# Forty matmuls that nobody reads, at four places of a one-core decoder layer

## The chip, the cores and the metric

The kernel runs on one core of a Trainium2 chip. The metric is the device time of one execution in microseconds (us). The kernel before was timed three times; the median is 1254.13 us (1252.01 to 1255.34). One further execution was profiled, and it is the one whose rows are quoted.

## The reference

One decoder layer on 1024 tokens of width 1024, all in float32. A mixer and a gated MLP follow each other, each between two RMS norms:

```python
h = _rms_norm(x, norm_pre_mix)
mix, v_first = _hybrid_mixer(h, ...)          # RWKV-7 heads beside a causal 31-tap convolution
x = x + _rms_norm(mix, norm_post_mix)
h = _rms_norm(x, norm_pre_ffn)
f = _conv_ffn(h, ...)                         # (gelu(conv3(h @ up)) * conv3(h @ up')) @ down
x = x + _rms_norm(f, norm_post_ffn)
...
# inside the mixer
p = h @ w_in                                  # 1024 -> 1024 (GLU) + 3 * 512 + small ones
y = _wkv7(r, decay, k, v, -kk, kk * a)        # a recurrence over the tokens, 8 heads of 64
c = silu(layer_norm(causal_dwconv(glu(u))))   # 512 channels, 31 taps
mix = concatenate([rwkv_out, c]) @ w_out      # 1024 -> 1024
```

## The kernel before, in words

The tokens are worked in two halves of 512, and the recurrence in four quarters of 256 (each four chunks of 64). Every matrix product with a weight is done as three matmuls on rounded parts: a weight tile is loaded by a DMA from SyncE's queue (line 184), ScalarE rounds it into `wh`, GpSimd subtracts to get `wl` (line 167), and TensorE accumulates `wh*hi`, `wh*lo` and `wl*hi` (lines 330 to 352). All matmuls go through one helper, so they carry line 140; transposes by TensorE carry line 155.

The program is written as streams with priorities (line 60): `rwkv` (1000) comes first, then `top` (the norm behind the first mixer half), `norm`, `conv` and last `proj` (the large products). A planner simulates all engines over time and lays out the order of every engine: at each moment an engine gets the ready instruction with the best priority. So `proj` matmuls fill the time that the recurrence leaves on TensorE. On the chip each engine then runs its list strictly in order, apart from weight loads. A matmul's accumulator is a PSUM bank taken by `bank(tag)`: there are two with the tag `pb`, two `pe`, one `pc`, and three fixed ones (`xs[0]`, `xs[1]`, `Y`). A bank is given out in rotation, and the next user waits until its last reader is done.

Four places matter here.

- **The second half's first transposes.** `channels` (line 273) takes four rows of 128 normalised tokens and turns them so that channels lie on partitions. For the second half it fills one bank per 128 channels: eight banks in turn, with tags pe, pb, pb, pe, pb, pb, pe, pb, four transposes of 128 columns each (line 287). ScalarE scales each bank into `hi` (line 292), VectorE makes `lo` (line 294), and that read frees the bank. After the eight banks stand the second half's first projections (`project(1, hs, "k0 k1 w r0 r1")`, line 1382). The first half runs the same helper with banks of two rows each.
- **The two output projections.** `w_out` (line 778) rounds the mixer's result into pairs (line 791), then makes four column blocks `ch` of 256. Each block uses two banks for 512 tokens and 96 matmuls of 256 columns. Block 0 uses `pb` banks, block 1 the banks `xs`. `evac` multiplies each bank into a tile (line 797), squares it for the norm's sum (ScalarE, line 803) and stores the tile to DRAM as `mixd` (line 805).
- **Behind the first output projection.** `w_out(0, ...)` is called at line 1394. The following `norm_ffn` (line 1400, stream `top`) loads `mixd` back in pieces into tiles `pt` (line 885), adds the residual (line 886), squares (line 887), and does its transposes as products with diagonal matrices `kk` in `pb` banks. At the same time the recurrence of the fourth quarter runs (`prepare(3)`). Its `bonus` (line 585) holds products with the constant block matrix in plain float32.
- **Ahead of the second output projection.** Nine products of the MLP's first matrix for the first half (`ffn_pair`, line 1410) fill TensorE up to `w_out(1, ...)` at line 1413. Their banks are read by `taps` (lines 910 to 919).

`self.lw` (line 249) is a constant of 96 partitions, written once near the start (ScalarE line 253, GpSimd line 255) and only read afterwards.

Of the kernel before, what the change touches and what calls it, by code (L numbers as in the profile page):

```python
# [22 lines left out]
P = 128  # L23
# [3 lines left out]
HALF = 512  # L27
# [73 lines left out]
class Trunk:  # L101
# [37 lines left out]
    def mm(self, out, lhsT, rhs, start=True, stop=True, skip=False):  # L139
        return self.nc.tensor.matmul(out, lhsT, rhs, start=start, stop=stop, skip_group_check=skip)  # L140

    def after(self, i, first):

        self.tc.add_manual_dep(
            i.ins, first.ins.name,
            mybir.DependencyInfo(mybir.DependencyClass.NoSync, mybir.DependencyReason.DATA),
            reason="the bank's first matmul clears it")
# [122 lines left out]
        self.ccarry = cp.tile([P, 4, 32], F32, name="ccarry")[:, :, :CONV_W - 1]  # L270


    def channels(self, rows, gname, hs, toks, tags=("pn",), diags=None):


        nc = self.nc
        n = len(rows) * P
        per = 512 // n
        for b, k0 in enumerate(range(0, KT, per)):
            ps = self.bank(tags[b % len(tags)])  # L280
            for i in range(per):
                k = k0 + i
                for t, row in enumerate(rows):
                    o = (k % 4) * P
                    out, src = ps[:, i * n + t * P:i * n + (t + 1) * P], row[k // 4][:, o:o + P]
                    if diags is None:
                        self.transpose(out, src)
                    else:
                        self.mm(out, src, diags[t])
            parts = [(self.par(gname, k0 + i), ps[:, i * n:(i + 1) * n], *hs[k0 + i]) for i in range(per)]  # L290
            for g, pv, hi, lo in parts:
                self.mark_hi = nc.scalar.activation(hi[:, toks], pv, AF.Copy, scale=g)
            for g, pv, hi, lo in parts:
                self.mark_lo = nc.vector.scalar_tensor_tensor(lo[:, toks], pv, g, hi[:, toks].bitcast(F32), ALU.mult, ALU.subtract)
# [483 lines left out]
    def w_out(self, h, mixr, co, behind=None):  # L778
        nc = self.nc
        if h == 0:  # L780
            acts = self.pairs("m")
        else:
            acts = []
            for _ in range(2):
                two = [self.tl("l8", [P, 4, HALF], F32R) for _ in range(2)]
                acts += [tuple(b[:, k] for b in two) for k in range(4)]
        with ExitStack() as gate:
            if behind is not None:
                gate.enter_context(self.tc.issue_after(behind.ins))
            for k in range(KT):  # L790
                self.split(*acts[k], mixr[:, k] if k < 4 else co[k - 4])

        def evac(ch, pss, post):
            for b, ps in enumerate(pss):
                o = self.tl("t2", [P, 512])
                with self.tc.high_priority():
                    nc.vector.tensor_tensor(  # L797
                        o.rearrange("p (t c) -> p t c", t=2), ps.rearrange("p (t c) -> p t c", t=2),
                        post.unsqueeze(1).broadcast_to([P, 2, 256]), ALU.mult)
                    for t in range(2):  # L800
                        tt = 4 * h + 2 * b + t
                        c = slice(t * 256, (t + 1) * 256)
                        nc.scalar.activation(ps[:, c], ps[:, c], AF.Square, accum_out=self.ssq[:, tt, ch:ch + 1])
                r = h * HALF + b * 256
                nc.sync.dma_start(
                    self.mixd[r:r + 256, ch * 256:(ch + 1) * 256].rearrange("(t p) c -> p t c", t=2),
                    o.rearrange("p (t c) -> p t c", t=2))

        for ch in range(4):
            post = self.tl("po", [P, 256])  # L810
            nc.sync.dma_start(post, self.a["post_mix"][:, ch * 256:(ch + 1) * 256].broadcast_to([P, 256]))
            pss = self.xs if ch == 1 else [self.bank("pe" if h and ch == 2 else "pb") for _ in range(2)]
            for k2 in range(KT // 2):
                wh, wl = self.weight(self.a["w_out"][ch, k2], [P, 2, 256], (self.mix, "ca", "ck") if h else None)
                if ch == 1 and k2 == 0:
                    mark = self.load
                for t in range(4):
                    for kk in range(2):
                        k = 2 * k2 + kk
                        hi, lo = acts[k]  # L820
                        s = slice(t * P, (t + 1) * P)
                        out = pss[t // 2][:, (t % 2) * 256:(t % 2 + 1) * 256]
                        start = k == 0 and t % 2 == 0
                        i = self.mm(out, hi[:, s], wh[:, kk], start=start, stop=False, skip=True)
                        if start:
                            first = i
                        elif k == 0 and kk == 0:
                            self.after(i, first)
                        self.mm(out, hi[:, s], wl[:, kk], start=False, stop=False, skip=True)
                        self.mm(out, lo[:, s], wh[:, kk], start=False, stop=k == KT - 1, skip=True)  # L830
            evac(ch, pss, post)
        return mark
# [26 lines left out]
    def norm_ffn(self, h, row, piece, hs, ahead=2, tags=("pn",), dg=None, pool=None):  # L859
# [38 lines left out]
        if ahead == 4:  # L898
            channels(0)
            yield  # L900
        channels(1)

    def taps(self, h, i, br, ps, acc):
# [219 lines left out]
    def ffn_down(self, acts):  # L1123
# [18 lines left out]
        def product(banks, src, wt, start, after, then=lambda j: None, held=(), soon=True):  # L1142
            ops, n = [], HT - len(held)
            for j in range(HT):
                with first():
                    hi, lo = self.pair("a", self.h1p)
                    self.split(hi, lo, src(j))
                    then(j)
                wh, wl = self.weight(wt(j), [P, 512], held=self.h1p if j % 2 else None) if j < n else held[j - n]
                op = (hi, wh), (hi, wl), (lo, wh)  # L1150
                if j >= n:
                    ops.append(op)
                else:
                    for t in range(4):
                        mms(banks[t], t, op, start and j == 0, j == HT - 1)

            ins = []
            for t in range(4):
                for i, op in enumerate(ops):
                    ins += mms(banks[t], t, op, False, i == len(held) - 1)  # L1160
                with first() if soon else ExitStack():
                    after(t)
            self.chain(ins)
# [101 lines left out]
    def mixer(self, sts):  # L1265
# [39 lines left out]
        def prepare(q):  # L1305

            c = lambda i: chunk(q - 1, i) if q else None
            f = lambda i: step(self.finish, q - 1, i, mixes[(q - 1) // 2]) if q else None

            c(0)  # L1310
            if q == 2:
                c(1)
                f(0)
            step(self.scores, q, 0)
            step(self.scores, q, 1)
            if q == 2:
                c(2)
                c(3)
                f(1)
                c = f = lambda i: None  # L1320
            c(1)
            step(self.keys, q)
            step(self.inverses, q)
            if q != 2:
                step(self.bonus, q)
            c(2)
            if q % 2:
                weave(self.merge(W[q]))
            c(3)
            f(0)  # L1330
            f(1)
            if q in (0, 2):
                weave(self.merge(W[q]), quarter(q + 1))
# [11 lines left out]

        def channels(rows, hs):
            with self.stream("norm"):
                self.channels(rows, "pre_mix", hs, slice(0, HALF), ("pe", "pb", "pb"))

        cut = lambda t: (t[:, :512], t[:, 512:])  # L1350
        with self.stream("norm"):
            two = [self.tl("l8", [P, 2, D]) for _ in range(2)]
            rows = [cut(two[t // 2][:, t % 2]) for t in range(4)]
            with self.stream("first"):
                self.load_rows(0, rows)
            hs = self.pairs("h")
# [7 lines left out]
        with self.stream("norm"):  # L1364
            two = self.tl("mixr", [P, 2, D])
            rows = [cut(two[:, t]) for t in range(2)]
# [10 lines left out]
        project(0, hs, "u2 u3")  # L1377
        hs = self.pairs("h")
        channels(rows, hs)
        mixes[0] = self.tl("mixr", [P, 4, HALF])  # L1380
        prepare(1)
# [10 lines left out]
        conv(1, 1, sts[0]["normed"])  # L1392
        with self.stream("proj"):
            self.w_out(0, mixes[0], [sts[0]["co", i] for i in range(4)])
        mixes[1] = self.tl("mixr", [P, 4, HALF])
        prepare(3)
        with self.stream("top"):
# [90 lines left out]
```

## Time and profile before

| | |
|---|---|
| timed executions | 1252.01, 1255.34, 1254.13 us; median 1254.13 us |
| the profiled execution | 1257.58 us, of which the span from first to last instruction is 1255.8 us |
| mean granted TensorE clock | 0.985 of full speed |
| TensorE matmul busy | 1210.4 us (96%), 8424 matmuls |
| VectorE, ScalarE, GpSimd busy | 899.8, 729.1, 507.1 us |

How to read the rows further below. Times are microseconds from the start of the span. A row of the timeline gives start, duration, engine (PE is TensorE, DVE VectorE, ACT ScalarE, POOL GpSimd, SPq the queue of SyncE), line, operation, output<-inputs by the program's names with buffer numbers left out, shape, and the number of instructions merged into the row. In brackets stands the idle time before it and who ended it. A row of the windows gives for a stretch of time its length, then for PE, PE's weight loads, DVE, ACT and POOL the busy time with the count of instructions, then the granted TensorE clock (1.00 is full), the share of the DMA engines, and GB/s. PE durations overlap, since matmuls are pipelined; what one matmul costs is the distance from start to start.

### The profile page before, as it was taken

Reading aid. Unit: us, or ns where it says so; the run is one execution under the profiler, and the core shown is the slowest. Engines: PE = TensorE matmul, PEld = TensorE weight load, DVE = VectorE, ACT = ScalarE, POOL = GpSimd, SP = SyncE. Lnnn points to the kernel's source line nnn. Section 1 sums busy time; section 2 is a strip of 40 time slices with the busy share of each in tenths; the row PEclk is TensorE's granted clock in tenths of the full one; section 3 lists DMA queues with packets and bytes.
Section 4 is the critical chain, followed back from the end, with each engine's and each line's share of the span. In section 5 each row is a group of like instructions: output and inputs, shape, how many; then the busy total and the mean of one; then the engine's idle time right before and its main releaser. Section 6 shows DMA issues by size and latency. Waiting matters only on the chain.

```text
span 1255.8 us, 22979 instructions
## 1 busy us (share of the span) xinstructions
PE 1210.4 (96%) x8424; PEld 988.9 (79%) x8424; DVE 899.8 (72%) x1558; ACT 729.1 (58%) x1515; POOL 507.1 (40%) x447
## 2 busy tenths in 40 slices
PE   5999999999999998999999999999999999999997
PEld 4767777787778876778889888888888888888885
DVE  5285998898669989998640555666656679479667
ACT  7563564565955676466762576876555566554451
POOL 4343330001103331344563399998888850000002
PEclk9999998999999989999999999999999999999999
DMA  7644442333343353222364798894322335336413
GB/s 243 177 131 137 129 135 64 97 128 119 114 128 91 97 178 110 75 80 85 104 186 118 271 323 293 298 315 153 82 74 81 101 134 166 95 117 219 134 52 134
DMA packets 102912, 180.97 MB, mean 144 GB/s; under 512 B 14896, under 2 KB 21424, under 8 KB 102800
## 3 DMA queue, kind: packets, MB, share of 16 engines
q1 hardware_dynamic: 102800, 179.51, 45.6%
q8 instruction: 66, 1.08, 0.4%
q14 instruction: 46, 0.38, 0.1%
HBM read 138.44 MB, written 41.03 MB: 143 GB/s over the span
## 4 chain that ended last, share of the span: by engine, by line
PE 62%; DVE 6%; ACT 2%; issue 1%; DMA 1%; POOL 1%; POOLq 0%; DVEq 0%; ACTq 0%
PE pb L140 27%; PE xs L140 16%; PE pe L140 14%; PE Y L140 2%; PE pc L140 2%; DVE pc L431 2%; DMA pt<-mixd 1%; PE pc L155 1%; PE pe L155 0%; DVE x L1120 0%; DVE m L167 0%; DVE sub L606 0%; DVE nrow L1136 0%; DVE dw L608 0%; DVE t L797 0%
## 5 line engine op out<-in xcount | busy, mean ns | idle before, releaser
L167 POOL TENSOR_TENSOR wl<-wr,wh 128x512 fp32r<-128x512 f32 (+1 forms) x175 | 230.0, 1316 | 219.4 <-ACT wh L167 191.3
L140 PE MATMUL pb<-h,wh 128*128 128x512 f32 (+3 forms) x720 | 230.1, 399 | 2.5 <-ACT wh L167 1.0
L167 ACT CAST wh<-wr 128x512 fp32r<-128x512 f32 (+1 forms) x214 | 131.4, 615 | 131.8 <-issue 42.3
L140 PE MATMUL pb<-f,wh 128*128 128x512 f32 x648 | 205.0, 397 | 2.7 <-ACT wh L167 1.7
L431 DVE SCALAR_TENSOR_TENSOR pc<-c,params,pc 128x512 f32<-128x512 f32 x232 | 174.2, 751 | 8.7 <-ACT pc L428 4.7
L140 PEld LDWEIGHTS pb<-h,wh 128*128 128x128 f32 (+2 forms) x720 | 132.1, 189 | 35.4 <-ACT wh L167 2.7
L140 PE MATMUL pb<-h,wl 128*128 128x512 f32 (+3 forms) x360 | 146.8, 408 | 2.3 <-POOL wl L167 2.1
L140 PEld LDWEIGHTS pb<-f,wh 128*128 128x128 f32 x648 | 121.8, 190 | 28.8 <-ACT wh L167 2.1
L140 PE MATMUL pb<-f,wl 128*128 128x512 f32 x324 | 129.2, 399 | 0.9 <-POOL wl L167 0.9
L162 POOL TENSOR_TENSOR ss<-var,mhalf 128x1 f32<-128x1 f32 x16 | 11.4, 716 | 223.8 <-DVE var L161 223.0
L1076 POOL TENSOR_TENSOR b<-b,b 128x512 f32<-128x512 f32 x72 | 93.3, 1298 | 1.9 <-DMA wr<-ffn_up 0.5
L140 PEld LDWEIGHTS pb<-h,wl 128*128 128x128 f32 (+2 forms) x360 | 67.8, 188 | 20.5 <-POOL wl L167 4.0
L140 PE MATMUL xs<-f,wh 128*128 128x512 f32 x240 | 74.2, 390 | 0.4 <-DVE act L973 0.4
L167 POOL TENSOR_TENSOR wl<-b,wh 128x512 fp32r<-128x512 f32 x48 | 66.6, 1388 | 16.9 <-ACT wh L167 14.9
L140 PEld LDWEIGHTS pb<-f,wl 128*128 128x128 f32 x324 | 61.7, 190 | 14.8 <-POOL wl L167 1.7
L167 ACT CAST wh<-b 128x512 fp32r<-128x512 f32 x48 | 29.7, 618 | 60.0 <-PE pb L140 20.5
L140 PE MATMUL pe<-f,wh 128*128 128x512 f32 x208 | 64.1, 389 | 0.0
L721 POOL TENSOR_TENSOR XG<-r,GE 64x256 f32<-64x256 f32 x30 | 20.5, 683 | 89.3 <-DVE r L740 84.5
L140 PEld LDWEIGHTS xs<-f,wh 128*128 128x128 f32 x240 | 44.9, 188 | 10.0 <-DVE act L973 0.8
L192 ACT CAST wh<-wr 128x512 fp32r<-128x512 f32 (+2 forms) x44 | 26.5, 604 | 44.4 <-PE pb L140 31.2
L167 ACT CAST a<-act 128x512 fp32r<-128x512 f32 x50 | 30.0, 620 | 33.6 <-PE Y L140 19.1
L167 ACT CAST w<-wr 128x512 fp32r<-128x512 f32 x38 | 23.4, 622 | 40.7 <-PE Y L140 20.0
(419 smaller groups left out, 2952.3 us busy)
## 6 DMA issues: line engine op xcount, KB each, us to landing
wr<-ffn_up SPq DMA_DIRECT2D x99, 256.0 KB, 3.2
wr<-w_in SPq DMA_DIRECT2D x80, 256.0 KB, 2.9
b<-ffn_up SPq DMA_DIRECT2D x52, 256.0 KB, 2.7
b<-ffn_down SPq DMA_DIRECT2D x44, 256.0 KB, 4.5
sums<-b SPq DMA_DIRECT2D x44, 256.0 KB, 4.2
wr<-sums SPq DMA_DIRECT2D x44, 256.0 KB, 2.8
lows<-wl SPq DMA_DIRECT2D x40, 256.0 KB, 3.3
wl<-lows SPq DMA_DIRECT2D x40, 256.0 KB, 2.7
```

Source lines behind the costliest of these rows:

```text
L140: return self.nc.tensor.matmul(out, lhsT, rhs, start=start, stop=stop, skip_group_check=skip)
L155: self.nc.tensor.transpose(out, in_, self.con("ident")[:n, :n])
L162: self.nc.gpsimd.tensor_tensor(out, v[:, :n], self.mhalf[:, :n], ALU.pow)
L167: return self.nc.scalar.copy(hi, src), eng.tensor_tensor(lo, src, hi.bitcast(F32), ALU.subtract)
L192: self.nc.scalar.copy(hi, raw)
L431: nc.vector.scalar_tensor_tensor(out, c[:, j:j + HALF], w(j), acc, ALU.mult, ALU.add)
L721: nc.gpsimd.tensor_tensor(x[64:128], R[64:128, gs], w.GE[64:128, c, gs].unsqueeze(2).broadcast_to([64, 4, CH]), ALU.mult)
L1076: sub = lambda o, x, y, op=ALU.subtract: self.nc.gpsimd.tensor_tensor(o, x, y, op)
```

## The change

A helper `busy(ps, n)` issues `n` matmuls into a bank: the stationary operand is `lw[:, 0, :128]` (96 by 128), the moving operand `lw[:, 0]` (96 by 512), both already on chip. Nobody reads what they write; the next real matmul of the same bank starts a new sum. They are put

- in `channels` for the second half, two ahead of each bank's four transposes (8 banks, 16 matmuls, stream `norm`);
- in `w_out`, six ahead of block 0, in its first bank, for both halves (12 matmuls, stream `proj`);
- behind `w_out(0, ...)`, four banks of the tag `pb` with three each (12 matmuls, stream `proj`).

Nothing is removed or moved by hand, and no DMA is added. Since the planner lays out all engines anew, other instructions can change places.

```diff
+    def busy(self, ps, n):
+
+        for _ in range(n):
+            self.mm(ps, self.lw[:, 0, :P], self.lw[:, 0], skip=True)
...
-    def channels(self, rows, gname, hs, toks, tags=("pn",), diags=None):
+    def channels(self, rows, gname, hs, toks, tags=("pn",), diags=None, busy=0):
...
             ps = self.bank(tags[b % len(tags)])
+            self.busy(ps, busy)
             for i in range(per):
...
             pss = self.xs if ch == 1 else [self.bank("pe" if h and ch == 2 else "pb") for _ in range(2)]
+            if ch == 0:
+                self.busy(pss[0], 6)
             for k2 in range(KT // 2):
...
-                self.channels(rows, "pre_mix", hs, slice(0, HALF), ("pe", "pb", "pb"))
+                self.channels(rows, "pre_mix", hs, slice(0, HALF), ("pe", "pb", "pb"), busy=2)
...
             self.w_out(0, mixes[0], [sts[0]["co", i] for i in range(4)])
+        with self.stream("proj"):
+            for _ in range(4):
+                self.busy(self.bank(), 3)
         mixes[1] = self.tl("mixr", [P, 4, HALF])
```

## The prediction

> **What bounds the kernel now.** I read the page first, then the chain, then a table of windows whose edges are the moments at which the granted clock changes, and last the timeline around each place of the change.
>
> ```profile
> span 1255.8 us, 22979 instructions
> ...
> PE 1210.4 (96%) x8424; PEld 988.9 (79%) x8424; DVE 899.8 (72%) x1558; ACT 729.1 (58%) x1515; POOL 507.1 (40%) x447
> ...
> PEclk9999998999999989999999999999999999999999
> ...
> PE 62%; DVE 6%; ACT 2%; issue 1%; DMA 1%; POOL 1%; POOLq 0%; DVEq 0%; ACTq 0%
> ```
>
> TensorE (PE) is busy nearly always and carries the chain, so 40 more matmuls are not free by themselves. The clock line has two dips below 9; this change can only pay there and in shorter dips that the slices blur. In the windows the number behind POOL's count is the clock:
>
> ```profile
> 183.01:186.42 3.41, 2.48 (x65) 1.96 (x58) 3.41 (x7) 3.31 (x8) 0.00 (x0) 1.00 0.74 226
> 186.42:189.84 3.42, 2.60 (x11) 1.76 (x12) 3.38 (x6) 3.26 (x7) 0.21 (x1) 0.50 0.02 5
> 189.84:193.25 3.41, 3.20 (x13) 2.40 (x13) 3.41 (x6) 0.97 (x2) 0.00 (x0) 0.50 0.00 0
> 193.25:196.66 3.41, 2.88 (x10) 2.30 (x10) 3.41 (x6) 2.14 (x4) 0.00 (x0) 0.50 0.00 0
> 196.66:200.07 3.41, 3.41 (x9) 2.64 (x9) 3.30 (x6) 0.00 (x0) 0.00 (x0) 0.50 0.00 0
> 387.81:391.22 3.41, 1.49 (x11) 1.28 (x12) 3.41 (x8) 2.23 (x6) 0.97 (x1) 1.00 0.27 77
> 391.22:394.63 3.41, 3.41 (x11) 2.38 (x12) 3.41 (x8) 3.41 (x8) 0.00 (x0) 0.50 0.00 0
> 456.08:459.49 3.41, 1.98 (x55) 1.67 (x53) 3.41 (x7) 2.80 (x8) 1.81 (x2) 1.00 0.58 153
> 459.49:462.91 3.42, 3.27 (x22) 1.67 (x24) 2.11 (x5) 3.31 (x11) 0.40 (x1) 0.50 0.96 296
> 462.91:466.31 3.40, 3.40 (x34) 2.04 (x32) 0.90 (x3) 1.38 (x5) 1.01 (x1) 0.50 0.83 276
> 469.72:473.13 3.41, 2.96 (x38) 2.23 (x40) 3.38 (x10) 2.00 (x7) 0.91 (x2) 1.00 0.87 287
> 633.56:636.98 3.42, 1.32 (x5) 0.80 (x6) 3.42 (x5) 2.99 (x7) 2.22 (x2) 1.00 0.24 77
> 636.98:640.39 3.41, 3.41 (x10) 2.64 (x9) 1.32 (x2) 1.97 (x3) 2.29 (x2) 0.50 0.60 171
> ```
>
> The clock is either full or half, and changes at steps of about 3.41 us. Each half-speed stretch stands behind a window in which PE had little wide work (1.32 to 2.48 us busy, the larger figures made of small tiles). It ends behind a window that is dense. Four such stretches lie near the four places of the change: 13.65 us, 3.41 us, 6.8 us and 3.41 us. At most half of that could be won, 13.6 us, and only where PE sets the pace.
>
> **The price of one added matmul.** Groups of three 512-column matmuls, at half and at full speed:
>
> ```profile
> 197.73 1.05 PE L140 MATMUL pb<-h,wh 128*128 128x512 f32 x2
> ...
> 199.01 1.05 PE L140 MATMUL pb<-h,wh 128*128 128x512 f32 x2
> ...
> 200.89 0.62 PE L140 MATMUL pb<-h,wh 128*128 128x512 f32 x2
> ...
> 201.58 0.39 PE L140 MATMUL pb<-h,wh 128*128 128x512 f32 x1
> ```
>
> Three take 199.01 - 197.73 = 1.28 us at half and 201.58 - 200.89 = 0.69 us at full speed: 0.43 and 0.23 us each. The added ones have 96 rows instead of 128; I take the same. All 40 cost 9.2 us of PE at full and 17.2 us at half speed. They issue no DMA and use no other engine, so what counts is where they stand in PE's order.
>
> **Part a, 16 at the second half's transposes.** Four transposes of a bank, and the last bank, at half and then at full speed:
>
> ```profile
> 190.96 0.69 PE L155 MATMUL pb<-const,mixr 128*128 128x128 f32 x2 [0.20 <-DVE h L294]
> ...
> 191.87 0.63 PE L155 MATMUL pb<-const,mixr 128*128 128x128 f32 x2
> ...
> 194.25 0.69 PE L155 MATMUL pb<-const,mixr 128*128 128x128 f32 x2 [0.53 <-DVE h L294]
> ...
> 195.02 1.20 PE L140 MATMUL pb<-h,wh 128*128 128x512 f32 x2
> ...
> 383.07 0.60 PE L155 MATMUL pe<-const,mixr 128*128 128x128 f32 x4
> 383.51 1.06 PE L140 MATMUL pe<-gd,lora 96*128 96x128 f32 x8
> ```
>
> At half speed a bank's four take 191.87 - 190.96 = 0.91 us, at full speed 383.51 - 383.07 = 0.44 us. Two fillers add 0.46 us at full speed, so a bank with its fillers takes 0.90 us: as long as now. Once the clock is up, the fillers cost nothing on the way from a bank's release (by VectorE, line 294) to ScalarE. What they buy is the first projection: from 195.02 to 200.07 four groups of three run at 1.28 instead of 0.69 us, 4 x 0.59 = 2.4 us. Against it: the first two banks meet a clock that is already down, 2 x 2 x 0.43 = 1.7 us. PE idles 0.93 + 0.82 = 1.75 us in the first two windows, but not only where the fillers stand; I count half of the price, 0.9 us. Part a gives -1.5 us. Its bounds: -2.4 us if all the price is hidden; for the bad end, the clock stays down (first rival).
>
> The half-speed windows 186.42 to 193.25 also tell why transposes do not bring the clock back: PE shows 2.60 and 3.20 us busy there, nearly all transposes, and the next window is still at 0.50. The Trainium skill, TensorE: Matmul & The Clock Gate, Part 4 (PE-mode transpose), says that transposes do not count as PE work for the clock in the way matmuls do; these two rows agree. The Trainium skill, same page, Part 1 (The HAM clock gate), speaks of a window of about 3.4 us that runs freely and of which one busy one is needed; the 3.41 us steps agree.
>
> Does the lead last? From 200 to 320 us PE has no idle time, so a projection that starts earlier moves everything behind it:
>
> ```profile
> 200.00:320.00 120.00, 120.00 (x1309) 93.50 (x1308) 101.46 (x189) 67.04 (x132) 12.70 (x21) 1.00 0.38 115
> ...
> 369.00:430.00 61.00, 57.94 (x613) 51.26 (x611) 59.06 (x111) 34.46 (x68) 17.67 (x17) 0.97 0.35 104
> ...
> 500.00:632.00 132.00, 131.48 (x1229) 105.85 (x1230) 112.51 (x183) 80.72 (x169) 57.54 (x47) 0.99 0.28 84
> ```
>
> From 369 to 430 VectorE leads (59.06 of 61 us), yet its work there waits for what PE projected before, so it can start earlier too.
>
> **Part b, six ahead of the first output projection.** Their bank was freed long before, they have the lowest priority, and the wait just ahead is this:
>
> ```profile
> 389.50 1.09 PE L155 MATMUL pe<-const,l 128*128 128x128 f32 x8 [2.19 <-DVE mixr L775]
> ```
>
> Six take 1.4 us and fit in 2.19 us. They may save the dip of 391.22 to 394.63, but VectorE is busy 3.41 of 3.41 us there and makes the operands that the projection waits for. I count 0. If the planner puts them behind that wait they cost up to 1.4 us; if the dip goes and PE sets the pace they win up to half of 3.41, 1.7 us.
>
> **Part c, twelve behind it.** The chain from 459.64 to 466.5 us is PE at half speed: small recurrence matmuls and two plain float32 products with the block matrix (`pt,const`). Then VectorE adds the norm's first piece:
>
> ```profile
> 460.89 0.20 ACT L803 ACTIVATION_READ_ACCUMULATOR pb<-pb 128x1 f32 x1
> ...
> 464.57 1.98 PE L140 MATMUL pe<-pt,const 128*128 128x512 f32 x2
> 466.48 0.48 PE L140 MATMUL pe<-l,l 64*128 64x128 f32 x2
> ...
> 496.78 1.88 PE L140 MATMUL pe<-pt,const 128*128 128x512 f32 x4
> ...
> 462.53 0.33 SPq L885 DMA_DIRECT2D pt<-mixd  x1
> ...
> 467.19 0.74 DVE L886 SCALAR_TENSOR_TENSOR row<-pt,nr,row 128x512 f32<-128x512 f32 x1
> ...
> DMA to landing us min/median/max: 2.7/3.1/4.2
> ```
>
> Two records take 466.48 - 464.57 = 1.9 us at half and 1.88 / 2 = 0.94 us at full speed. The first freed bank is free at 460.89 + 0.20 = 461.1 us, so these fillers cannot keep the clock from falling at 459.49; three of them may lift the window to 462.91 enough to end the stretch one step early. That would halve 462.91 to 466.31 (3.40 us), 1.7 us. The next limit is the load of `mixd`, issued at 462.53 and landing 3.1 us later at 465.6, against 467.19 now: 1.6 us. I take -1.6 us. From there to 500 us the chain is loads and VectorE, so the gain is kept. The other nine fall into PE's waits between 467 and 500, ahead of the norm's transposes in the same banks. If the first three stand ahead of the recurrence and the clock stays down, they cost 3 x 0.43 = 1.3 us and win nothing; if all twelve do, at full speed 12 x 0.23 = 2.8 us.
>
> **Part d, six ahead of the second output projection.**
>
> ```profile
> 636.81 1.52 DVE L919 SCALAR_TENSOR_TENSOR pt<-pb,params,pt 128x511 f32<-128x511 f32 x2
> ...
> 640.34 11.71 PE L140 MATMUL pb<-wm,l 128*128 128x256 f32 x96
> ```
>
> The bank of these six is read by `taps` until 636.81 + 1.52 = 638.3 us, behind the wait that pulls the clock down (the window from 633.56). From 636.98 to 640.39 PE is full. So they land directly ahead of the projection at 640.34, which waits for nothing: +1.4 us, at half speed 2.6 us, and 0 only if a wait opens there. No half-speed stretch is shortened.
>
> **Sum.** -1.5 + 0 - 1.6 + 1.4 = -1.7 us. The profiled execution takes 1257.6 us (1255.8 of span and 1.8 around it), so it would be 1255.9. It lies 3.5 us above the median of 1254.1; the same difference gives **1252.4 us**. About 0.3%, 3.8 us, is what a measurement of this kernel can tell from no change, so this counts as the same. The planner's new order is a cost of either sign that no row prices; it is why the forecast's own spread is -5 to +2 us around no change.
>
> **Rivals.** *The clock stays down and the fillers stand in the way (slower).* Place: 184 to 195 us. Six fillers in the window 189.84 to 193.25 are 2.6 us of wide work at half speed. The window from 193.25 had 196.66 - 195.02 = 1.6 us of dense matmuls and was not enough; one with 3.40 us busy (462.91) was. The point is whether 2.6 of 3.41 suffices. If not, 16 x 0.43 = 6.9 us less the idle 0.93 + 0.82 + 0.21 + 0.53 = 2.5 us is +4.4 us, with part d's 1.4 it is +5.8: 1259.9 us. By the Trainium skill, TensorE: Matmul & The Clock Gate, Part 1 (The HAM clock gate), a sustained busy window is needed, which speaks for this rival. Against it: the full clock survived 469.72 to 473.13 on small tiles. Chance 0.20.
>
> *The clock is held at all of a, b and c (faster).* Then 2.4 us from a, 1.7 from b, and in c half of the 6.7 us busy from 459.49 to 466.31, 3.3 us, if the load of `mixd` moves up as well; less 1.4: -6.0 us, 1248.1 us. For it speaks that PE has no idle time behind a; against it that c's bank comes free too late in this profile. Chance 0.25.
>
> *The gain is hidden.* VectorE between 369 and 430 and the loads behind 467 absorb a and c, and +1.4 us of d remains: 1255.5 us. Matmuls that the build drops as unread, or that the planner puts in waits, end here too: 1254 us. Chance 0.12.
>
> **The numbers.** Forecast 0.43, rivals 0.20, 0.25, 0.12. Faster by over 0.3%: the second rival and a quarter of the forecast's spread, 0.25 + 0.11 = 0.36. Slower: the first rival and a rest of 0.02, 0.22. The same: 0.42. The forecast's own range is 1249 to 1256; with the rivals' prices it reaches from 1246 to 1260.
>
> **What would show it.** Right: the clock is full from about 193 us on, the first projection's groups of three take 0.69 us, the bank turns stay near 0.9 us, the stretch behind 459 us is one step shorter, and 1.4 us of fillers stand directly ahead of the second output projection. Wrong: the stretch at 186 us lasts as long with fillers 0.43 us each in it; the norm's first addition does not move against the end of the first output projection; or the stages between the four places change their length, which would be the planner's order and not the clock.

## The result, and the profile after

The changed kernel takes 1259.88 us (median of 19 runs, 1255.89 to 1262.98), the kernel before 1253.62 us beside it (19 runs, 1252.01 to 1257.67). The ratio is 1.0042, 95% interval 1.0034 to 1.0051: slower, by more than the 0.3% that can be told from no change. The medians are 6.3 us apart; the ratio, which is that of the means, gives 5.3 us (4.3 to 6.4). The forecast was 1252.4 us and "the same". Three executions among the runs below took far longer (1341.59, 1981.69 and 2370.96 us); the ratios leave them out.

The profiled execution of the changed kernel took 1259.5 us. Its page, with the span, the busy times, the clock and the shares of the chain:

```profile
span 1257.6 us, 23060 instructions
...
PE 1214.6 (97%) x8464; PEld 991.7 (79%) x8464; DVE 899.5 (72%) x1558; ACT 730.6 (58%) x1515; POOL 506.6 (40%) x447
...
PEclk9999999999999999999999999999999999999998
...
PE 61%; DVE 7%; DMA 2%; ACT 1%; issue 1%; POOL 1%; DVEq 0%; POOLq 0%; SPq 0%; ACTq 0%
```

The dips of the clock line are gone, so the clock did come up. PE is busy 4.2 us longer, and the span is longer too. The windows between the clock's own steps show where it still fell (the number behind POOL's count is the clock):

```profile
189.51:192.92 3.41, 1.69 (x10) 1.12 (x9) 3.37 (x6) 1.25 (x3) 0.00 (x0) 1.00 0.00 0
192.92:196.33 3.41, 3.41 (x13) 2.57 (x12) 3.41 (x6) 0.93 (x2) 0.00 (x0) 0.50 0.00 0
196.33:199.75 3.42, 3.42 (x17) 2.69 (x17) 3.13 (x6) 2.19 (x4) 0.00 (x0) 1.00 0.00 0
391.40:394.80 3.40, 3.28 (x21) 2.22 (x19) 3.40 (x9) 3.15 (x8) 0.00 (x0) 1.00 0.09 35
421.61:425.02 3.41, 3.41 (x18) 3.07 (x16) 3.30 (x6) 3.35 (x8) 0.54 (x1) 0.50 0.68 128
462.61:466.02 3.41, 3.41 (x15) 1.64 (x16) 1.61 (x5) 2.62 (x9) 0.19 (x1) 0.50 0.88 273
636.60:640.00 3.40, 3.40 (x17) 2.82 (x16) 1.09 (x2) 3.39 (x9) 1.38 (x2) 1.00 0.50 156
```

The 13.65 us at half speed from 186 us have become one step of 3.41 us. The stretches at 391 and 637 us are gone. New ones stand at 421 and 480 us. That part a ends the stretch at 186 us does not rest on one profile: between 180 and 205 us the ten profiles without part a have 6.9 to 13.7 us at half speed (eight of them 13.7), the seven with its fillers as they are or narrowed have 0 to 3.4 us. In all, the half-speed time between 50 us and the last few us went from 34 to 13.7 us in these two profiles. Over the timed runs the median clock rose from 0.988 (35 executions of before, timed beside the single parts) to 0.992, that is (0.012 - 0.008) x 2 x 1254 = 10 us less at half speed, worth 5 us of PE's time at most. Against it stand forty fillers, at least 40 x 0.23 = 9.2 us.

The fillers of part a, and the first projection behind them (timeline of PE, changed kernel):

```profile
185.07 0.73 PE L140 MATMUL pb<-lw 96*128 96x512 f32 x2 [0.22 <-ACT t L420]
...
191.24 0.73 PE L140 MATMUL pe<-lw 96*128 96x512 f32 x2 [1.58 <-DVE h L300]
...
194.00 1.20 PE L140 MATMUL pb<-lw 96*128 96x512 f32 x2
...
197.61 0.73 PE L140 MATMUL pb<-h,wh 128*128 128x512 f32 x2
...
198.41 0.63 PE L140 MATMUL pb<-h,wh 128*128 128x512 f32 x2
...
199.10 0.62 PE L140 MATMUL pb<-h,wh 128*128 128x512 f32 x2
```

The groups of three take 199.10 - 198.41 = 0.69 us from the start, as forecast, but the first one comes at 197.61 instead of 195.02 us. The six of part b stand around the gate projection's last matmuls, ahead of the transposes and of the wait for `mixr`:

```profile
384.58 0.94 PE L140 MATMUL pb<-lw 96*128 96x512 f32 x3
...
387.70 0.87 PE L140 MATMUL pb<-lw 96*128 96x512 f32 x3
388.40 0.60 PE L160 MATMUL pe<-const,l 128*128 128x128 f32 x4
390.38 0.66 PE L160 MATMUL pe<-const,l 128*128 128x128 f32 x4 [1.38 <-DVE mixr L781]
```

And the six of part d directly ahead of the second output projection:

```profile
640.07 1.52 PE L140 MATMUL pb<-lw 96*128 96x512 f32 x6
641.43 3.75 PE L140 MATMUL pb<-wm,l 128*128 128x256 f32 x30
```

They take 641.43 - 640.07 = 1.36 us there, the 1.4 us of the forecast.

**How two traces are laid against each other.** Below, "the shift" is the start of the same PE instruction (same tiles and shape, same place in the order of such instructions) in one profile less its start in the profile of before, as a median of fifteen neighbours, counted from 100 us on. At 175, 210, 404, 452 and 660 us it reads (us):

```
kernel                175    210    404    452    660
the whole change      0.0   -0.6   -0.9   +0.9   +0.6
a alone               0.0   -1.0   +0.3   +0.3   +0.1
a alone, again       -0.1   -0.6   +0.8   +0.8   -1.6
b alone               0.0   -0.2   -0.5   +1.0   -0.5
c alone               0.0   -0.9   -1.4   -1.3   -0.6
d alone               0.0   -0.5   -0.8   -0.8   -0.7
```

The profile of before took 1257.6 us, 3.5 us over the median, and a kernel without any filler at 186 us also gains against it there: between 175 and 210 us the eight kernels without part a that keep the order of before up to there (before itself among them, at 0) shift by +0.1 to -0.9 us, -0.4 us in the mean. A shift within a stretch says where something happens; how much the change costs on average is told by the timed runs alone.

### The profile page after: what moved, and what is told of

Read it like the earlier page. It is cut to its first block, busy times and chain, and to the rows that moved or that the text cites. A ratio compares the mean times of both kernels' runs of the same rounds, so it can differ in the third digit from the quotient of the medians.

```text
span 1257.6 us, 23060 instructions
## 1 busy us (share of the span) xinstructions
PE 1214.6 (97%) x8464; PEld 991.7 (79%) x8464; DVE 899.5 (72%) x1558; ACT 730.6 (58%) x1515; POOL 506.6 (40%) x447
## 4 chain that ended last, share of the span: by engine, by line
PE 61%; DVE 7%; DMA 2%; ACT 1%; issue 1%; POOL 1%; DVEq 0%; POOLq 0%; SPq 0%; ACTq 0%
PE pb L140 26%; PE xs L140 16%; PE pe L140 14%; PE Y L140 2%; PE pc L140 2%; DVE pc L437 2%; DMA pt<-mixd 1%; PE pc L160 1%; DMA mixd<-t 1%; DVE x L1128 0%; DVE dw L614 0%; PE pe L160 0%; DVE m L172 0%; DMA row<-x 0%; DVE l L570 0%
```

## The experiments

Theory A: PE is the pace, and a filler costs the time that it keeps PE or what waits for PE, wherever it stands; the clock gives less back. Theory B: the cost is the planner's new order. The changed kernel has hundreds of PE and VectorE instructions in other places than before, nearly all of them because of part c.

**Each part alone.** Four kernels, each with one of the four places kept (three shown as the lines that differ from the changed kernel):

```diff
 a alone
-                self.busy(pss[0], 6)
-            for _ in range(4):
-                self.busy(self.bank(), 3)
 b alone
-                self.busy(pss[0], 6)
+                self.busy(pss[0], (6, 0)[h])
...
 d alone
-                self.busy(pss[0], 6)
+                self.busy(pss[0], (0, 6)[h])
...
```

a alone:

> Only the 16 matmuls at the second half's transposes; the planner's order is otherwise that of before (8 of 1572 VectorE instructions and 4 matmuls change places). Fillers in the way: the clock gained does not pay for them, 16 x 0.23 = 3.7 us less what lies beside waits, +2 to +4.5 us. The clock pays: the stretch of half speed behind 186 us goes from four steps to one or none, -0.5 to -2.5 us. New order: nothing, within 1 us of before.

b alone:

> Only the six ahead of the first output projection; few instructions change places (46 matmuls, 20 of VectorE, 12 of ScalarE). Fillers in the way: in the profile after, everything from 430 to 455 us is 1.5 us later than it was at 380, so +1.4 us. Free beside the wait, as predicted: within 0.5 us of before. New order: within 1 us.

c alone:

> Only the twelve behind the first output projection. With them the planner lays out 460 to 640 us anew (378 of 6830 matmuls, 241 of VectorE's, 150 of ScalarE's instructions change places). New order: most of the 6 us lost comes here, +3 to +6 us. Fillers in the way: at most 12 x 0.23 = 2.8 us, and less beside waits, +0.5 to +2.8 us. As predicted: -1.6 us.

d alone:

> Only the six ahead of the second output projection; 24 matmuls change places, nothing on VectorE, ScalarE or GpSimd. As predicted and by fillers in the way: six times 0.23 = +1.4 us, +2.6 if the clock is down there. New order: nothing.

Measured, against 1254.05 us of before on the same chip (35 runs):

| kernel | median us | ratio | 95% interval | PE, VectorE instructions moved |
|---|---|---|---|---|
| a alone | 1255.63 | 1.0014 | 1.0001 to 1.0028 | 4, 8 |
| b alone | 1256.68 | 1.0018 | 1.0003 to 1.0033 | 46, 20 |
| c alone | 1253.68 | 1.0001 | 0.9989 to 1.0014 | 378, 241 |
| d alone | 1256.44 | 1.0017 | 1.0003 to 1.0031 | 24, 0 |

The four add up to 1.0050, within the interval of the whole (1.0034 to 1.0051). Part c, which brings nearly the whole of the new order, costs nothing that can be told, its twelve fillers included (-1.4 to +1.8 us); a, b and d, which move little, cost about 2 us each. As the account of this change, theory B falls. That an order can be dear is shown further down.

**Part d, six and eighteen.** Three times the fillers at the same place. In the profiles the other instructions of PE, VectorE, ScalarE and GpSimd keep the order of before, with eighteen as with six; a few DMA issues change places.

```diff
-                self.busy(pss[0], (0, 6)[h])
+                self.busy(pss[0], (0, 18)[h])
```

> Part d alone with 18 added matmuls in place of 6 ahead of the second output projection; every other engine has the order that d with 6 had. Theory A (an added matmul costs the time it keeps PE, 0.23 us at full clock, since the projection behind it is on the chain): 18 x 0.23 = 4.1 us over the kernel before, 2.8 over d with 6, so near 1258. Theory B (the cost is the moved instructions and the shifted waits, whatever the number): as d with 6, 2.2 us over before, near 1256.5. Theory C (they hold the clock in the 632 to 640 us stretch and more of them hold it better): less than d with 6.

Measured: 1258.06 us against 1253.82, ratio 1.0035 (1.0023 to 1.0046), some +4.3 us where theory A had +4.1 and B +2.2. The timeline of PE shows it directly, d alone:

```profile
637.79 2.38 PE L140 MATMUL pb<-lw 96*128 96x512 f32 x6
640.01 10.24 PE L140 MATMUL pb<-wm,l 128*128 128x256 f32 x84
```

and with eighteen:

```profile
638.52 5.10 PE L140 MATMUL pb<-lw 96*128 96x512 f32 x18
643.46 6.75 PE L140 MATMUL pb<-wm,l 128*128 128x256 f32 x55
```

Six keep the projection back by 640.01 - 637.79 = 2.22 us, eighteen by 643.46 - 638.52 = 4.94 us. The first ones run in the half-speed stretch, which was 632.8 to 639.6 us in d alone, so six cost 0.37 us each rather than 0.23. The clock there did not profit. Part d is settled: its price is its time on PE, on the path.

**Part b, narrow and moved.** The same six, at the same place, cut to almost nothing:

```diff
-            self.mm(ps, self.lw[:, 0, :P], self.lw[:, 0], skip=True)
+            self.mm(ps[:32, :16], self.lw[:, 0, :32], self.lw[:, 0, :16], skip=True)
```

> Part b alone, six added matmuls in the same place, each cut to 32 stationary and 16 moving columns. Theory A (the time on PE is the cost): some 0.06 us each, 0.4 us in all, so within 0.5 us of the kernel before instead of 2.4 over it. Theory B (the cost is the order that the planner makes when anything stands there): about 2 us over before, as with the wide ones.

Measured: 1254.85 us, ratio 1.0004 (0.9994 to 1.0015), against 1.0018 (1.0003 to 1.0033) with the wide ones. That speaks for theory A; the two intervals overlap, so this pair alone does not close it. Where the time goes is seen in the rows of before:

```profile
386.01 0.63 PE L140 MATMUL pb<-h,wh 128*96 128x512 f32 x2
...
386.72 0.62 ACT L167 CAST wh<-wr 128x512 fp32r<-128x512 f32 x1 [1.50 <-issue]
...
387.41 1.36 POOL L167 TENSOR_TENSOR wl<-wr,wh 128x512 fp32r<-128x512 f32 x1 [2.82 <-ACT wh L167]
...
388.23 0.62 DVE L606 TENSOR_TENSOR sub<-dw 128x50 f32<-128x50 f32 x1
...
388.77 0.68 DVE L775 TENSOR_TENSOR mixr<-mixr,pe 128x512 f32<-128x512 f32 x1
...
417.95 0.68 DVE L797 TENSOR_TENSOR t<-xs,po 128x512 f32<-128x512 f32 x1
...
419.92 0.28 PEld L155 LDWEIGHTS xs<-const,v 128*64 128x64 f32 x2 [0.50 <-ACT xs L803]
```

and in those of b alone (line numbers are 5 or 6 higher there):

```profile
386.85 0.63 PE L140 MATMUL pb<-h,wh 128*96 128x512 f32 x2
...
387.56 0.62 ACT L172 CAST wh<-wr 128x512 fp32r<-128x512 f32 x1 [2.23 <-issue]
...
388.26 1.26 POOL L172 TENSOR_TENSOR wl<-wr,wh 128x512 fp32r<-128x512 f32 x1 [3.55 <-ACT wh L172]
388.35 1.25 DVE L612 TENSOR_TENSOR sub<-dw 128x50 f32<-128x50 f32 x1
...
389.51 0.68 DVE L781 TENSOR_TENSOR mixr<-mixr,pe 128x512 f32<-128x512 f32 x1
...
419.21 0.69 DVE L803 TENSOR_TENSOR t<-xs,po 128x512 f32<-128x512 f32 x1
...
421.18 0.41 PE L160 MATMUL xs<-const,v 128*64 128x128 f32 x2 [1.11 <-DVE t L803]
```

Ahead of the fillers the two are 0.1 us apart. VectorE's multiplication into `mixr` comes 389.51 - 388.77 = 0.74 us later. Its other input, `pe`, is the product with `lora`, which both kernels have made ahead of the fillers (383.51 and 383.63 us); it reads nothing of the transposes that stand behind them (at 388.26 instead of 386.70 us). What holds it is the short `sub` update in front of it, 0.20 us long where GpSimd is idle: it takes 0.62 us in before and 1.25 us here, until GpSimd's subtraction ends, at 387.41 + 1.36 = 388.77 and 388.26 + 1.26 = 389.52 us. That subtraction waits for ScalarE's cast into `wh`, and the cast begins 0.08 us behind the end of the gate projection's last `h,wh` matmuls in both (386.64 and 387.48 us); that it waits for them is inferred from this. Three of the six fillers stand ahead of these matmuls, at 384.44 us in b alone. So the delay goes from PE by way of ScalarE and GpSimd to VectorE. From there VectorE has no room (59.06 of 61 us busy, in the prediction) and falls 1.26 us behind by 419.21 - 417.95. At 421 us PE waits 1.11 us for VectorE's `t`; in before its weight load had waited 0.50 us for ScalarE there. The changed kernel has the same 1.11 us wait, and its shift rises from -0.9 to +0.9 us between 404 and 452 us. With the narrow fillers the multiplication is less than 0.1 us late, against 0.6 us here (the distance ahead of the fillers taken off both), yet VectorE falls behind by some 0.8 us up to 418 us too, so a part of that is the order; PE is 0.8 us late at 404 us as well in that one profile, and yet the timed runs show no cost.

The wide six tied behind the gate projection's last matmul:

```diff
-    def busy(self, ps, n):
...
+    def busy(self, ps, n, behind=None):
+        for i in [self.mm(ps, self.lw[:, 0, :P], self.lw[:, 0], skip=True) for _ in range(n)]:
+            if behind is not None:
+                self.after(i, behind)
...
+                self.busy(pss[0], (6, 0)[h], self.gate)
...
+        project(1, hs, "v0 v1 g"); self.gate = self.last
```

> Part b alone with its six wide matmuls tied behind the gate projection's last matmul, so that they stand ahead of the wait for mixr (2.19 us before) and no longer between the gate projection's matmuls. Theory A with cover: the 1.4 us of PE lie under that wait, within 0.5 us of the kernel before. Without cover (the transposes that follow are themselves what the wait is for): 1.4 to 2.4 us over before, as b. The planner also moves some 420 PE instructions behind it, which c, with 378 moved, did at no cost.

Measured: 1261.57 us, ratio 1.0062 (1.0048 to 1.0075), +7.7 us. Neither value came. The planner's order changed by some 420 PE instructions, and the profile loses 8.5 us between 404 and 452 us, far more than six fillers, and gets a part back later. So an order that the planner makes anew is not always free as it was with c; this run cannot say what its six fillers cost. It is a miss.

**Part a, a second time.** The same kernel as a alone, for a second sample.

> Part a alone a second time, for a second profile. Theory A (part a costs by itself, somewhere): again 1.0 to 2.0 us over before, though its own stretch, 175 to 210 us, was 0.6 to 1.0 us shorter in three profiles with part a. If the loss of the first profile (a GpSimd subtraction of 4.89 us at 396, after which PE waited 2.13 us) is what costs, it is there again at 396 to 401. Theory B (part a costs nothing; the 1.0014 was chance): within 0.5 us of before.

Measured: 1255.37 us against 1253.45, ratio 1.0014 (1.0002 to 1.0026). Both samples of part a lie above before, each with an interval that begins just above 1. In its own stretch part a does gain (shift -1.0 and -0.6 us at 210, -0.6 in the changed kernel). Both profiles of a alone lose it at the same place, behind 396 us. Before:

```profile
396.62 1.28 DVE L167 TENSOR_TENSOR m<-co,m 128x512 fp32r<-128x512 f32 x2
397.69 1.37 POOL L167 TENSOR_TENSOR wl<-wr,wh 128x512 fp32r<-128x512 f32 x1 [8.91 <-ACT wh L167]
...
399.06 1.28 DVE L167 TENSOR_TENSOR m<-co,m 128x512 fp32r<-128x512 f32 x2
```

a alone:

```profile
395.97 6.14 POOL L172 TENSOR_TENSOR wl<-wr,wh 128x512 fp32r<-128x512 f32 x2 [7.35 <-ACT wh L172]
396.47 1.28 DVE L172 TENSOR_TENSOR m<-co,m 128x512 fp32r<-128x512 f32 x2
...
398.45 1.28 DVE L172 TENSOR_TENSOR m<-co,m 128x512 fp32r<-128x512 f32 x2
...
400.91 0.39 PE L140 MATMUL pb<-wl,m 128*128 128x256 f32 x1 [2.13 <-POOL wl L172]
```

a alone, again:

```profile
396.93 5.28 POOL L172 TENSOR_TENSOR wl<-wr,wh 128x512 fp32r<-128x512 f32 x2 [8.28 <-ACT wh L172]
...
401.02 0.39 PE L140 MATMUL pb<-wl,m 128*128 128x256 f32 x1 [1.75 <-POOL wl L172]
```

GpSimd's subtraction for a weight tile starts 0.8 to 1.7 us earlier, beside VectorE's subtractions instead of at the end of the first two. Each row holds two of them. The view by tile has their shortest and longest (ns), of a alone:

```profile
L172 POOL TENSOR_TENSOR wl<-wr,wh x2: 1282/3086/4891, 396.0 to 400.8; 128x512 fp32r<-128x512 f32 x2
```

and of a alone, again:

```profile
L172 POOL TENSOR_TENSOR wl<-wr,wh x2: 1280/2658/4035, 396.9 to 400.9; 128x512 fp32r<-128x512 f32 x2
```

So the first lasted 4.9 and 4.0 us instead of 1.37, and ended 1.1 and 1.2 us behind VectorE's last `m<-co`. PE waits 2.13 and 1.75 us for it. In these two profiles what was gained is given back, and more. The changed kernel's own profile does not show it: the subtraction takes 1.58 us at 397.62 us, PE does not wait for it, and the shift is still -0.9 us at 404 us.

**Part a with a quarter of the array.** The 16 fillers with 32 stationary columns and 512 moving ones: same order, same time on PE.

```diff
-            self.mm(ps, self.lw[:, 0, :P], self.lw[:, 0], skip=True)
+            self.mm(ps[:32, :512], self.lw[:, 0, :32], self.lw[:, 0, :512], skip=True)
```

> Part a alone with the 16 added matmuls cut to 32 stationary columns and still 512 moving ones: the same order of the instructions as a and the same time on PE, but a quarter of the array's columns. If the clock follows how long PE is busy: no half-speed stretch from 186 to 200 us, the mean clock stays near 0.992 and the time near that of a (1.6 us over before). If it follows how much of the array works: the half-speed stretch of before is there again, the mean clock falls to 0.988, and the 16 run at half clock for 0.43 us each, so 3 us or more over before.

Measured: 1254.66 us, ratio 1.0012 (1.0001 to 1.0023); one half-speed step of 3.4 us at 191.9 us, as the changed kernel has one at 192.9. In this profile the clock follows how long PE is busy, not how many columns work. The twelve timed runs do not settle it: their median clock is 0.990, between the two values expected, and that of before beside them 0.989.

**Part a, with each filler four times as long.** The 16 in plain f32, which PE runs as two records each, 0.43 to 0.46 us from start to start at full speed:

```diff
-            self.mm(ps, self.lw[:, 0, :P], self.lw[:, 0], skip=True)
+            self.mm(ps, self.lw[:, 0, :P].bitcast(F32), self.lw[:, 0].bitcast(F32), skip=True)
```

> Part a alone with the 16 added matmuls in plain f32 in place of fp32r, which makes each longer on PE (by the f32 matmuls with a full row of 512 in the other profiles some 0.5 to 0.9 us against 0.23). If VectorE sets the pace from 183 to 197 us, so that PE has room there, the stretch from 175 to 210 us grows by less than half of the added PE time. If PE sets it, by all of it: 4 to 11 us later at 210 us.

Measured: 1264.83 us, ratio 1.0087 (1.0073 to 1.0100). The rows of PE:

```profile
185.38 1.98 PE L140 MATMUL pb<-lw 96*128 96x512 f32 x4
187.20 0.38 PE L160 MATMUL pb<-const,mixr 128*128 128x128 f32 x2
```

A bank's two fillers take 187.20 - 185.38 = 1.82 us instead of some 0.57, and in two banks that fell into a half-speed stretch 3.5 and 3.0 us. In all eight banks it is 17.2 us against 4.5 us in a alone, 12.7 us more. The stretch from 175 to 210 us is 9.6 us longer than in before, so 10.6 us longer than in a alone (10.2 than in its second profile). Five sixths of the added time are on the path: beyond what a has, PE has no room there, though VectorE was busy 16.92 of 17.06 us in before. At this slope the 4.5 us of part a cost 3.8 us, an estimate that takes the first filler to cost what the added ones do. In its profiles a alone is 0.2 to 0.6 us ahead of the mean of the kernels without it (-0.6 and -1.0 against -0.4), so by this estimate the clock gives back that price and hardly more.

**Combinations.** All but a, and a with c:

```diff
 all but a
-                self.channels(rows, "pre_mix", hs, slice(0, HALF), ("pe", "pb", "pb"), busy=2)
+                self.channels(rows, "pre_mix", hs, slice(0, HALF), ("pe", "pb", "pb"), busy=0)
 a with c
-                self.busy(pss[0], 6)
```

> Parts b, c and d without a. If the parts add up (b 2.4, c 0, d 2.2): 4.6 us over before, 1.0035. If a matters in the whole as it does alone, 1.5 us below the whole change (1.0042), so again 1.003 to 1.0035. If a's clock gain pays once b, c and d are there (half-speed stretch at 186 back, nothing else): as the whole change or above it, 1.0042 or more.

> Parts a and c, without the matmuls ahead of the two output projections (b and d). If b and d are what costs: as a alone, within 1.5 us of before (1.0000 to 1.0013). If the cost comes from c's new order together with the others: 3 us or more over before.

Measured: all but a 1258.39 us, ratio 1.0034 (1.0021 to 1.0046), as the sum of b, c and d has it; against the whole (1.0042) that leaves about 1 us for part a, less than the intervals can tell. a with c 1256.07 us against 1253.45, ratio 1.0025 (1.0015 to 1.0035), about 3 us: above the 1.5 us expected from a alone, at the edge of the other expectation. The two alone add up to 1.0015, and the intervals overlap. No combination is faster than before.

**Does the GpSimd subtraction carry a's loss?** Two pairs of kernels, each pair with the same new order and apart by part a alone. The subtraction of the first output projection's third weight tile is made by VectorE in the first pair, those of the third and the fourth in the second (first pair shown; its three statements stand in one line of the kernel):

```diff
+                pool, self.low_pool = self.low_pool, self.low_pool and not (h == 0 and ch == 0 and k2 in (2,))
                 wh, wl = self.weight(...)
+                self.low_pool = pool
```

> The kernel before with one thing changed: the subtraction that makes the low half of the first output projection's third weight tile (the GpSimd instruction at 397 us) goes to VectorE. The planner moves some 420 PE instructions for it, so its distance to before is not read; it is the base for the next run, which differs from it by part a alone.

> The same with part a. Theory A (a's loss is the stretched GpSimd subtraction at 397 us, which is gone here): at or below the run without a, by 0 to 1 us. Theory B (a's loss is elsewhere): 1.3 to 2 us above it, as part a over before.

> As the first, with the third and the fourth weight tile's subtractions on VectorE: the base of a second pair, in another order of the planner's.

> The same with part a. Theory A: at or below the run without a, by 0 to 1 us. Theory B: 1.3 to 2 us above it.

Measured against 1254.68 us of before: first pair 1258.79 without (ratio 1.0028, 1.0017 to 1.0040) and 1259.03 with a (1.0032, 1.0021 to 1.0043); second pair 1262.20 without (1.0053, 1.0038 to 1.0068) and 1260.83 with a (1.0042, 1.0027 to 1.0058). With the subtraction away, a adds 0.2 us and -1.4 us (medians), where it added 1.6 and 1.9 us alone. The first difference lies between the two expectations, nearer to A; the second is A's. It speaks for the GpSimd subtraction as a carrier of a's loss. It does not show it: the intervals of each pair overlap, and a with 32 columns and a with c have that subtraction at 1.9 us in their one profile, without a wait of PE, and are over before all the same. Whether their other executions fall into it stays open. And the two bases lie 4.1 and 7.5 us over before, although VectorE got only one or two subtractions more. All five kernels with such a dear order, these four and the one with the tied fillers, lose at one place in their profiles: between 430 and 452 us the shift grows by 6.7 to 7.8 us, PE waits 2.9 to 3.6 us for ScalarE's `l` (line 672), and 3.4 to 6.9 us at half speed begin at 440 to 442 us. No other profile has either. So the price of an order is here that of one wait and of the clock behind it; why these orders open the wait stays open.

## Why the prediction was wrong

- **The clock.** Right as a mechanism: groups of three at 0.69 us, the stretch at 186 us ended early, that at 391 us gone. First rival (the clock stays down) did not happen, though its 1259.9 us is nearly the time measured. The agreement is chance.
- **Part a, "-1.5 us".** Measured +1.6 and +1.9 us alone. Two steps failed. "I count half of the price, 0.9 us": by the slope of the longer fillers some 3.8 us are on PE's path, and the clock gives back some 4 us, not 2.4 (both estimates). The forecast reckoned that a bank with its fillers at full speed takes as long as one without at half speed, and saw idle time as cover; but PE at full speed had to come back behind VectorE (1.58 us ahead of 191.24), and the fillers lay behind that wait, not in it. And "a projection that starts earlier moves everything behind it" held only to 396 us: there the earlier ScalarE and GpSimd work met VectorE's, and PE waited 2.13 and 1.75 us in the two profiles of a alone. How much of part a's cost this wait carries on average stays open; the changed kernel's profile is without it.
- **Part b, "I count 0".** Measured +2.3 us (0.18% of 1254). "Six take 1.4 us and fit in 2.19 us" took a wait as room without asking what ends it. `mixr` was waited for, and its maker, VectorE, was held by GpSimd's subtraction, which followed, by way of ScalarE, gate matmuls that now stood behind three of the fillers. The wait shrank from 2.19 to 1.38 us, the result came 0.74 us later, and VectorE carried the delay to 421 us. That the transposes behind the fillers are what the wait is for, as an expectation above has it, is not so: the multiplication into `mixr` does not read them.
- **Part c, "-1.6 us".** Measured +0.1 us, -1.4 to +1.8. The bank comes free late, as said, and three fillers stand at 459.99 us. In c alone the clock holds from 456 to 474 us but falls later for as long:

```profile
462.80:466.20 3.40, 3.40 (x33) 2.34 (x32) 2.19 (x3) 1.12 (x4) 1.01 (x1) 1.00 0.62 202
...
469.60:474.70 5.10, 2.61 (x23) 1.94 (x24) 3.32 (x9) 1.70 (x5) 0.61 (x1) 1.00 0.23 71
...
478.10:484.90 6.80, 6.80 (x61) 6.12 (x62) 4.08 (x12) 3.64 (x10) 0.55 (x1) 0.50 0.46 157
```

  PE idles 5.10 - 2.61 = 2.5 us at 470 us, in the recurrence's new place, and 10.2 us at half speed follow it. Before had 6.8 us at 459.5 and 3.4 us at 514.1, 10.2 us as well. "The gain is kept" named one stretch and not the next one.
- **Part d, "+1.4 us".** Right in kind and place; the size is 1.36 us in the changed kernel and 2.2 us alone, where the fillers run in the half-speed stretch, between the 1.4 and the 2.6 us that were given.
- **The sum.** With the measured parts 1.8 + 2.3 + 0.1 + 2.1 = 6.3 us, each its ratio times 1254, against 5.3 us (4.3 to 6.4) of the whole by its ratio. A frame would have given most of it: PE busy 96% of the span and 62% of the chain, forty fillers of 0.23 us are 9.2 us of work, and the half-speed time saved returns at most half of itself, 5 us.
- **The chances.** Slower had 0.22 and hung on one rival whose mechanism did not come. The planner's order, named as a cost "of either sign", was near 0 with part c, but 4 to 8 us in three of the experiments; a spread of -5 to +2 us was a guess in the wrong direction.

## What to carry to other kernels

Where one engine is busy nearly all the time, an added instruction on it costs its full time until a row shows the contrary; a half-speed stretch that ends returns at most half its length, and only where that engine sets the pace. Before a wait counts as cover, follow what ends it: work put ahead of the wait delays it if the awaited result, or an engine that its maker must wait for, hangs on something behind that work. A dose (three times the fillers, or the same ones narrow) on an otherwise unchanged order separates an instruction's own price from that of the order around it, which one run with and one run without cannot.

## What the runs showed of the hardware that was not expected

- A GpSimd subtraction of 128x512 that takes 1.37 us when it begins at the end of VectorE's first two `m<-co` subtractions took 4.9 and 4.0 us when it began 0.5 us ahead of them or 0.4 us into them. The Trainium skill, SBUF — State Buffer, section "SBUF: two separate sides", says that GpSimd and VectorE share a pair of ports as an exclusive lock: a GpSimd instruction, or a VectorE instruction with two inputs in SBUF, holds it to its end while the other is fully blocked. By that rule GpSimd waits out VectorE's subtractions; that the slow ones end only behind VectorE's last `m<-co` agrees. The rule does not say why GpSimd stayed out between the two pairs as well, where VectorE ran `pc<-c,params,pc` for 0.74 us, with one input in PSUM. The reverse is seen too: in before VectorE's small `dw` update at 398.49 us, 0.20 us long where GpSimd is idle, takes 0.65 us until GpSimd is through at 399.06, and most of part b's 0.74 us at 388 us is made in this way.
- In the one profile taken, fillers that use a quarter of the array's columns end the half-speed stretch like full ones (one step of 3.4 us left, as in the changed kernel). The Trainium skill, TensorE: Matmul & The Clock Gate, Part 1 (The HAM clock gate), speaks of how busy PE is in a window of time; this agrees.
- The clock's steps fall differently in each execution. Two executions of the same kernel, a alone, had their steps near 461 us as 6.8 us at 460.6 and at 460.9, but one had a half-speed step at 191 and at 389 us and the other had neither. A single profile is one draw; what a change costs on average is read from the timed runs.
